# Four edits to the scans of a state-space layer: the order of sums, products, loads and splits

## The chip, the cores and the metric

The kernel runs on one core of a Trainium2 chip. The metric is the device time of one execution in microseconds (us). A profile of one execution gives each engine's instructions with start and duration. The engines are TensorE (PE), VectorE (DVE), ScalarE (ACT), GpSimd (POOL) and SyncE (SP, which here issues most of the DMAs). Each takes its own instructions strictly in order.

## The reference, cut to what matters

One inference step of two layers, a Mamba-2 layer and a pooling layer, over 1024 prompt tokens and 64 sample tokens (8 sequences of 8), in float32. The scans belong to the first layer:

```python
acum = jnp.cumsum(dt * A, axis=2)                         # per head, within chunks of 128 tokens
decay = where(mask, exp(acum[t] - acum[s]), 0)
y_intra = (C B^T * decay) @ (x * dt)                      # the rows of a chunk
chunk_states = B^T @ (x * dt * exp(acum[-1] - acum))      # what a chunk adds to the state
h_next = exp(acum[-1]) * h + chunk_states
y_inter = C @ h_prev * exp(acum)
y = y_intra + y_inter + d_skip * x
gated = y * silu(z)                                       # then normalised within each of 8 groups
gated = gated * rsqrt(mean(gated ** 2) + eps) * norm_g
out = gated @ w_out                                       # 2048 -> 1024
```

The 32 heads form 8 groups of 4 that share `B` and `C`. The prompt begins with a state of zero; each of the 8 sample sequences has a state of its own, read, used and returned.

## The kernel before, in words

All tensors lie feature-major: 128 features on the partitions, 1088 columns (1024 prompt tokens, 64 sample tokens). A product in nearly full precision takes three matmuls: each operand is split into a rounded part (`hh`, `wh`, `gh`) and a rest (`hl`, `wl`, `gl`). ScalarE makes the rounded part, VectorE the rest: for weights L141 and L145, for the out-projection's input `op_split`, L782 and L783.

The program has three stretches. The **front** (to about 348 us) has the normalisation, the modulation and a part of the in-projection; early in it the cumulative decays go to a DRAM tensor `acd`. Then **`ssd_layer`** runs eight scans, one for each group 0 to 7 (to about 925 us). Last comes the rest of the out-projection's layer and the pooling layer.

A scan is the generator `scan_group` (L521 ff.). For each of eight chunks of 128 tokens `front(c)` loads the decay of chunk c+2 into one of three `acb` tiles (`load_ac`, L549), broadcast to all partitions, 256 KB each; transposes `x` and `B` on TensorE into a bank `tr` (L573, L576); makes the decay matrix `M` on ScalarE, four times L581 and then an exponential L582, the row factor `ea` (L565), `cd` (L601), and `Bt`, the rounded transpose of `B` (L593). For each pair of chunks `states` makes the chunk states (`S`, L615) and `rows` the outputs (L637, L641), which VectorE adds to `x` (`evac_y`, L607). Chunk 8 is the sample: `sample_inter` multiplies the sample's `C` with the old states (`Z`, L656) and VectorE scales this (`zsc`, L659); `back_sample` adds to it on POOL (L665), multiplies with `M` (L670), and POOL scales the old states (L674, twice); `state_sample` makes four products `S[0]` to `S[3]` (L692), in banks of the kinds `S`, `y`, `y` and `tr`, and VectorE adds them to the states (L695, four times). Then come the products with `z` (L732), their squares on ScalarE (L733), the sum of the two squares on VectorE (`zsum`, L769), and in the scan's next step the row sums on TensorE (`ms`, L741). PSUM has two `tr` banks, two `y`, one `S` and three `mm`.

Between two steps of a scan, other work fills TensorE's queue, by a table `FILL` of unit counts: in the groups 0 to 4 units of the in-projection for the next groups (groups 1, 2, 3, 4 and 6, three `mm` banks evicted by ScalarE, L434 and L436, followed by a convolution over four taps, L366 to L372, most of it on VectorE), then units of the out-projection (`op_first`, L807 to L812). The very last in-projection unit (`proj_group`, group 6, part 3) also takes steps of a generator `prep`, each of which loads rows `gr` for the out-projection and splits the rows loaded before. A scheduler places the instructions on the engines by priority and readiness, so a changed order in the code can change it in a neighbouring place.

Of the kernel before, what the change touches and what calls it, by code (L numbers as in the profile page):

```python
# [11 lines left out]
ALU = mybir.AluOpType  # L12
# [3 lines left out]
P = 128  # L16
# [83 lines left out]
class Build:  # L100
# [296 lines left out]
    def proj_group(self, G):  # L397

        for ii in range(4):
            w = self.stream_next()  # L400
            raw = self.proj_begin(G, ii)
            if (G["g"], ii) == (BESIDE[-1], 3):

                ps = [self.mm_tile() for _ in CH]
                for k in range(8):
                    for c, j in ((0, k), (1, k), (2, 0), (2, k)) if k == 1 else ((0, k), (1, k), (2, k))[:3 if k else 2]:
                        self.mm1(ps[c], w, j, self.hn[j], CH[c], j == 0, j == 7)
                    for j in (0, 1) if k == 1 else (k,) if k else ():
                        self.slots.free(*self.hn[j])
                    if 0 < k < 5:  # L410
                        next(self.prep)
                    elif k in ():
                        self.load_x(0, k - 0)
                    if k < 7:
                        yield
                for c in range(3):
                    self.proj_evict(G, ii, raw, ps[c], c, False)
                next(self.prep)
                yield
                self.late = lambda: self.proj_end(G, ii, raw, True)  # L420
                return
            ada = self.ada_do(self.ada_plan[G["g"], ii]) if (G["g"], ii) in self.ada_plan else iter(())
            for c in range(3):
                ps = self.mm_tile()
                self.mm3(ps, w, self.hn, CH[c])
                self.proj_evict(G, ii, raw, ps, c)
                if c != (0, 0, 2, 0)[ii]:
                    next(ada, None)
                yield
# [95 lines left out]
    def scan_group(self, g, T):  # L525
        nc, tk, gp, pp = self.nc, self.tk, self.gs, self.pp
        B, C, xs, zs = T[0], T[1], T[2:4], []
        hsl, h0 = [], []

        def load_z():  # L530
            for q in range(2):
                zs.append(self.slots.get("z"))
                nc.sync.dma_start(zs[q], self.zsd[2 * g + q])

        def load_h0():
            for i in range(2):
                t = self.slots.get("h0")
                nc.sync.dma_start(t[:, :1024], self.io["h0T"][g][:, 1024 * i:1024 * i + 1024])
                hsl.append(t)
                h0.append(t[:, :1024].rearrange("p (b r q) -> p b r q", b=4, r=4))  # L540

        h = [None]
        acbs = {}

        def load_ac(c):
            if c < 8:
                j, cc = c // 2, c % 2
                t = gp.tile([P, 4, 128], F32, tag="acb", bufs=3, name=self.name("acb"))
                nc.sync.dma_start(t, self.acd[32 * j + 4 * g:32 * j + 4 * g + 4, 128 * cc:128 * cc + 128].unsqueeze(0).to_broadcast([P, 4, 128]))  # L549
            else:  # L550
                t = gp.tile([P, 4, 128], F32, tag="acb", bufs=3, name=self.name("acb"))[:, :, :64]
                nc.sync.dma_start(t, self.acd[96 + 4 * g:100 + 4 * g, 256:320].unsqueeze(0).to_broadcast([P, 4, 64]))
            acbs[c] = t
# [133 lines left out]
        def state_sample(xm, Bt):  # L687
            S = [pp.tile([P, 512], F32, tag=t, bufs=b, name=self.name("S")) for t, b in (("S", 1), ("y", 2), ("y", 2), ("tr", 2))]
            for i in range(2):
                for j in range(4):  # L690
                    o = slice(32 * j, 32 * j + 32)
                    nc.tensor.matmul(S[j], Bt[i][o, :], xm[o, :], start=(i == 0), stop=(i == 1), tile_position=(32 * j, 0))  # L692
            for j in (3, 2, 1, 0):
                d = hsl[j // 2][:, 512 * (j % 2):512 * (j % 2) + 512]
                nc.vector.tensor_tensor(out=d, in0=d, in1=S[j], op=ALU.add)  # L695
            for i in range(2):
                nc.sync.dma_start(self.io["hsT"][g][:, 1024 * i:1024 * i + 1024], hsl[i][:, :1024])
                self.slots.free(hsl[i])

        load_ac(0)  # L700
        load_ac(1)
        F = [front(0)]
        yield
        F.append(front(1))
        yield
        for c in range(0, 8, 2):
            states(c, F)
            if c == 6:
                load_z()
            Fn = [front(c + 2)]  # L710
            if c == 6:
                self.slots.free(B)
            yield
            rows(c, F)
            F = Fn
            if c < 6:
                F.append(front(c + 3))
                if c == 4:
                    load_h0()
            else:  # L720
                zsc = sample_inter()
                self.slots.free(C)
            yield
        F, h = F[0], h[-1]
        nc.sync.dma_start(self.io["hpT"][g], h.rearrange("p r q -> p (r q)"))
        st = back_sample(F, zsc)
        yield
        state_sample(*st)

        sq = zs  # L730
        for q in range(2):
# [1 line left out]
            nc.scalar.activation(sq[q], xs[q], AF.Square)  # L733
        self.zadd = functools.partial(nc.vector.tensor_tensor, out=sq[0], in0=sq[0], in1=sq[1], op=ALU.add)
        if g not in (5, 6):
            self.zsum()
        yield
        self.zsum()
        ps = self.pp.tile([P, 512], F32, tag="y", bufs=2, name=self.name("ms"))
# [745 lines left out]
    def front_pairs(self, ops, dt):  # L1485

        nc, sl = self.nc, self.slots
        self.fast_init(len(FRONT))
        self.G, G, ends = {}, None, []

        def end(G, g, ii, ts):
            for i in range(2):
                self.proj_end(G, ii + i, ts[i])
                if g:
                    t = G["out"].pop()
                    nc.sync.dma_start(self.xbd[g][ii + i], t)
                    sl.free(t)

        for n, (kind, g) in enumerate(FRONT):
            if kind == "z":  # L1500
                ts = [sl.get("z") for _ in range(2)]
                outs = [(t, 0, None) for t in ts]
            else:
                if kind == "b":
                    self.G[g] = G = self.proj_open(g)
                ii = 2 * (kind == "x")
                ts = [self.proj_begin(G, ii + i) for i in range(2)]
                outs = [(t, 3, t[:, 1027:1115].rearrange("p (b w) -> p b w", w=11)[:, :, 3:11]) for t in ts]

            def after(x):  # L1510
                if kind == "z" and x in ("z01", "z11"):
                    a = HALF * int(x[1])
                    self.z_chunk(ts[1], ts[1][:, a:a + HALF], a, HALF)
                elif kind == "z" and x in ("B21", "B22"):
                    a = HALF * (x == "B22")
                    ins = self.z_chunk(ts[0], ts[0][:, a:a + HALF], a, HALF)
                    if n == len(FRONT) - 1 and x == "B22":
                        with self.tc.issue_after(ins.ins):
                            t = self.mt.tile([P, NS], F32, tag="gs", bufs=2, name=self.name("gs"))
                            nc.scalar.activation(t[:, :1], self.eps, AF.Exp)  # L1520
                    if x == "B22":
                        self.gate_store(2 * g, ts[0])
                elif kind == "z" and x == "T4":
                    self.gate_store(2 * g + 1, ts[1])
                if x == "B21":
                    while ends:
                        ends.pop(0)()
                if kind != "z" and x == "B22":
                    ends.append(functools.partial(end, G, g, ii, ts))
                if n == 0 and x in ("B11", "B21"):  # L1530
                    next(ops)
                if n < 2 and x in ("B21", "T3", "T4"):
                    next(dt, None)
                if n == len(FRONT) - 1:
                    if x in ("T2", "T3"):
                        sl.free(*[self.T[int(x[1]), k] for k in range(4)])
                    elif x == "T1":
                        for k in range(4):
                            for i in range(2):
                                nc.sync.dma_start(self.hn[k][i][:, HALF:].bitcast(F32), self.b12d[2 * k + i])  # L1540

            self.fast_pair(*outs, after)
        for f in ends:
            f()
        sl.free(*[self.T[4, k] for k in range(4)])
# [366 lines left out]
```

## Time and profile before

| what | value |
| --- | --- |
| median of 3 runs | 1600.0 us (1599.32 to 1602.75) |
| the profiled execution's own time | 1601.08 us |
| its span in the trace | 1599.3 us |
| TensorE busy | 1572.6 us, 98% |
| VectorE, ScalarE, GpSimd busy | 81%, 49%, 32% |
| scans | about 348 to 925 us |

In rows of the timeline the columns are the start, the time to the end of the last of them, engine, line, operation, output and inputs, shapes, and how many were put together; in brackets stands the idle time of the engine before it and what ended that. In the list of waits each row names the engine and the operation that waited, the operation it waited for, the total, how often and the longest.

### The profile page before, as it was taken

The page shows a single profiled execution, that of the slowest core. Times are in us where ns is not written, and L with a number is a line of the kernel's source. Part 1 is how long each engine was busy: PE and PEld are TensorE (multiplying, and loading weights), DVE is VectorE, ACT ScalarE, POOL GpSimd, SP SyncE. Part 2 cuts the span into 40 slices and gives each one's busy share as a digit, 9 for nine tenths or more (in the row PEclk, how much of TensorE's full clock was granted, in tenths as well). Part 3 has the DMA queues.
Part 4 walks back from the last instruction along what each step waited for, and adds up shares of the span by engine and source line. Part 5 has one row for each costly group of instructions (what it writes and reads, how often), then busy time and mean ns, then how long its engine had stood idle before and what let it go on. Part 6 is the DMA issues. An engine that isn't in the chain of part 4 may idle for free.

```text
span 1599.3 us, 30704 instructions
## 1 busy us (share of the span) xinstructions
PE 1572.6 (98%) x11946; PEld 1505.4 (94%) x11946; DVE 1299.5 (81%) x2152; ACT 790.2 (49%) x1512; POOL 514.1 (32%) x558
## 2 busy tenths in 40 slices
PE   9999999999999999999999999999999999999997
PEld 7899999999898988888998999999999999999997
DVE  6874879778888888889888868998889777667886
ACT  6663344357666666675555437533332233233364
POOL 0133556512322313141211232375666630000241
PEclk9999999999999999999999999999999999999999
DMA  9422232355555654579989532232333379566683
GB/s 353 166 100 108 72 112 83 110 179 170 174 161 166 179 182 145 207 246 321 310 325 319 191 135 73 66 136 102 116 112 110 104 248 366 140 180 180 161 171 116
DMA packets 122306, 275.59 MB, mean 172 GB/s; under 512 B 18192, under 2 KB 59312, under 8 KB 122160
## 3 DMA queue, kind: packets, MB, share of 16 engines
q1 hardware_dynamic: 118128, 260.90, 47.7%
q0 software_dynamic: 4032, 12.72, 4.6%
q8 instruction: 94, 1.54, 0.4%
q14 instruction: 52, 0.43, 0.1%
HBM read 201.12 MB, written 70.23 MB: 170 GB/s over the span
## 4 chain that ended last, share of the span: by engine, by line
PE 79%; DVE 9%; issue 4%; ACT 4%; DMA 2%; POOL 1%; SPq 0%; DVEq 0%; ACTq 0%; POOLq 0%
PE st L1053 10%; PE st L1051 10%; PE st L1052 10%; PE mm L190 10%; PE mm L191 10%; PE mm L192 9%; PE op L1270 2%; PE op L1271 2%; PE op L1269 2%; PE S L615 2%; PE y L637 2%; DMA acb<-acd 1%; PE tr L576 1%; PE am L261 1%; PE tr L573 1%
## 5 line engine op out<-in xcount | busy, mean ns | idle before, releaser
L1051 PE MATMUL st<-hh,w 128*128 128x272 f32 x832 | 240.3, 289 | 0.9 <-ACT w L182 0.9
L1053 PE MATMUL st<-hh,w 128*128 128x272 f32 x832 | 240.4, 289 | 0.4 <-DVE w L184 0.4
L1052 PE MATMUL st<-hl,w 128*128 128x272 f32 x832 | 239.9, 288 | 0.0
L1051 PE MATMUL st<-t,w 128*128 128x272 f32 x624 | 179.6, 288 | 0.0
L1053 PE MATMUL st<-t,w 128*128 128x272 f32 x624 | 179.5, 288 | 0.0
L1052 PE MATMUL st<-t,w 128*128 128x272 f32 x624 | 179.2, 287 | 0.0
L190 PE MATMUL mm<-hh,wh 128*128 128x368 f32 (+1 forms) x528 | 178.2, 337 | 0.0
L191 PE MATMUL mm<-hl,wh 128*128 128x368 f32 (+1 forms) x528 | 174.8, 331 | 0.0
L192 PE MATMUL mm<-hh,wl 128*128 128x368 f32 (+1 forms) x528 | 173.2, 328 | 0.0
L1051 PEld LDWEIGHTS st<-hh,w 128*128 128x128 f32 x832 | 156.7, 188 | 1.3 <-ACT w L182 1.3
L1053 PEld LDWEIGHTS st<-hh,w 128*128 128x128 f32 x832 | 156.4, 188 | 0.9 <-DVE w L184 0.9
L1052 PEld LDWEIGHTS st<-hl,w 128*128 128x128 f32 x832 | 156.7, 188 | 0.0
L182 ACT ACTIVATE w<-wr 128x512 fp32r<-128x512 f32 x104 | 64.9, 629 | 166.4 <-PE st L1053 137.4
L623 POOL TENSOR_TENSOR hd<-h,cd 128x256 f32<-128x256 f32 x56 | 47.5, 849 | 303.2 <-DVE h L624 142.1
L1270 PE MATMUL op<-b,w 128*128 128x272 f32 x448 | 128.9, 288 | 1.0 <-DVE b L1199 1.0
L1269 PE MATMUL op<-b,w 128*128 128x272 f32 x448 | 129.4, 289 | 0.0
L1271 PE MATMUL op<-b,w 128*128 128x272 f32 x448 | 129.0, 288 | 0.1
L190 PE MATMUL mm<-gh,wh 128*128 128x368 f32 (+1 forms) x372 | 125.5, 338 | 0.0
L192 PE MATMUL mm<-gh,wl 128*128 128x368 f32 (+1 forms) x372 | 122.1, 328 | 0.0
L191 PE MATMUL mm<-gl,wh 128*128 128x368 f32 (+1 forms) x372 | 121.9, 328 | 0.1
L1051 PEld LDWEIGHTS st<-t,w 128*128 128x128 f32 x624 | 117.7, 189 | 0.1
L1053 PEld LDWEIGHTS st<-t,w 128*128 128x128 f32 x624 | 117.3, 188 | 0.0
(307 smaller groups left out, 4578.1 us busy)
## 6 DMA issues: line engine op xcount, KB each, us to landing
wr<-win SPq DMA_DIRECT2D x48, 512.0 KB, 3.6
acb<-acd SPq DMA_DIRECT2D x64, 256.0 KB, 4.4
wr<-pin SPq DMA_DIRECT2D x32, 512.0 KB, 3.7
wr<-pout SPq DMA_DIRECT2D x28, 512.0 KB, 5.4
x<-x1d SPq DMA_DIRECT2D x24, 544.0 KB, 6.0
x1d<-x SPq DMA_DIRECT2D x22, 544.0 KB, 4.3
wr<-pout POOLq DMA_DIRECT2D x20, 512.0 KB, 5.6
x<-xT SPq DMA_DIRECT2D x16, 544.0 KB, 6.3
```

What stands on the lines that cost most here:

```text
L182: self.nc.scalar.activation(hi, src, AF.Copy)
L190: nc.tensor.matmul(ps[:, :n], hi[:, k, :], ah[:, a:a + n], start=first, stop=False)
L191: nc.tensor.matmul(ps[:, :n], hi[:, k, :], al[:, a:a + n], start=False, stop=False)
L192: nc.tensor.matmul(ps[:, :n], lo[:, k, :], ah[:, a:a + n], start=False, stop=last)
L615: nc.tensor.matmul(S[:, 256 * i:256 * i + 256], Bt, xde.rearrange("p r q -> p (r q)"), start=True, stop=True)
L623: nc.gpsimd.tensor_tensor(out=hd, in0=h[-1], in1=cd.unsqueeze(2).to_broadcast([P, 4, 64]), op=ALU.mult)
L1051: nc.tensor.matmul(ps[c][:, :QUART], hi[:, k], xh[:, t], start=(k == 0), stop=False)
L1052: nc.tensor.matmul(ps[c][:, :QUART], hi[:, k], xl[:, t], start=False, stop=False)
L1053: nc.tensor.matmul(ps[c][:, :QUART], lo[:, k], xh[:, t], start=False, stop=(k == 3))
L1269: nc.tensor.matmul(ps[:, :QUART], hi[:, k], xh, start=k == 0, stop=False)
L1270: nc.tensor.matmul(ps[:, :QUART], hi[:, k], xl, start=False, stop=False)
L1271: nc.tensor.matmul(ps[:, :QUART], lo[:, k], xh, start=False, stop=k == 7)
```

## The change

Four things change, with no effect on what is computed.

1. In a scan, the sum of the two squares (`zsum`) is issued only after the last of the four additions to the sample's state has been placed (all groups but 5 and 6, where it already came later).
2. `sample_inter`, the product of the sample's `C` with the old states, is emitted ahead of the rows of the chunks 6 and 7 and no longer behind them.
3. The decays of the chunks 0 and 1 of scan 0 are loaded within the front into a slot `acs`, as soon as the last product of the front has given up some of its tiles; the scan then starts with chunk 2's load. The slot is given back after `front(1)`.
4. In the last in-projection unit (group 6, part 3), one step of `prep` moves from between the matmuls to behind the evictions.

```diff
@@ proj_group
-                    if 0 < k < 5:
+                    if 0 < k < 4:
                         next(self.prep)
...
                 for c in range(3):
                     self.proj_evict(G, ii, raw, ps[c], c, False)
+                next(self.prep)
                 next(self.prep)
                 yield
@@ state_sample
             for j in (3, 2, 1, 0):
                 d = hsl[j // 2][:, 512 * (j % 2):512 * (j % 2) + 512]
-                nc.vector.tensor_tensor(out=d, in0=d, in1=S[j], op=ALU.add)
+                ins = nc.vector.tensor_tensor(out=d, in0=d, in1=S[j], op=ALU.add)
...
+            return ins
@@ scan_group
-        load_ac(0)
-        load_ac(1)
+        acbs.update(self.ac01)
+        self.ac01 = {}
+        for c in range(2):
+            if c not in acbs:
+                load_ac(c)
         F = [front(0)]
         yield
         F.append(front(1))
+        if self.acsl is not None:
+            self.slots.free(self.acsl)
+            self.acsl = None
...
+            if c == 6:
+                zsc = sample_inter()
+                self.slots.free(C)
             rows(c, F)
...
-            else:
-                zsc = sample_inter()
-                self.slots.free(C)
...
-        state_sample(*st)
+        added = state_sample(*st)
...
         if g not in (5, 6):
-            self.zsum()
+            self.zsum(added)
@@ front_pairs, after product T3 of the last pair
+                        if x == "T3":
+                            self.acsl = t = sl.get("acs")
+                            self.ac01 = {c: t[:, 512 * c:512 * c + 512].rearrange("p (r t) -> p r t", r=4) for c in range(2)}
+                            for c in range(2):
+                                nc.sync.dma_start(self.ac01[c], self.acd[0:4, 128 * c:128 * c + 128].unsqueeze(0).to_broadcast([P, 4, 128]))
```

Three places in the engines' orders follow. The line numbers of the changed kernel are higher by 1 from L418 on and by 8 from L732 on.

VectorE at the end of group 3, before (`ea` is the row factor of a later group's chunk, `h` the sample's states, `S` the four products with `S_7552` to `S_7555` for `S[0]` to `S[3]`, `z` the squares, `wl` a weight's rest):

```order
L602 TENSOR_TENSOR ea_7834<-xbc_7167,ea_7834 128x512
L769 TENSOR_TENSOR z_7356<-z_7356,z_7358 128x1088
L695 TENSOR_TENSOR h_117_7313<-h_117_7313,S_7555 128x512
L695 TENSOR_TENSOR h_117_7313<-h_117_7313,S_7554 128x512
L695 TENSOR_TENSOR h_116_7311<-h_116_7311,S_7553 128x512
L695 TENSOR_TENSOR h_116_7311<-h_116_7311,S_7552 128x512
L280 TENSOR_SCALAR shf_275<-am_7541,vec 128x9
```

and now (`S_7551` to `S_7554` for `S[0]` to `S[3]`):

```order
L603 TENSOR_TENSOR ea_7833<-xbc_7166,ea_7833 128x512
L696 TENSOR_TENSOR h_117_7310<-h_117_7310,S_7551 128x512
L696 TENSOR_TENSOR h_118_7312<-h_118_7312,S_7553 128x512
L696 TENSOR_TENSOR h_118_7312<-h_118_7312,S_7554 128x512
L696 TENSOR_TENSOR h_117_7310<-h_117_7310,S_7552 128x512
L777 TENSOR_TENSOR z_7355<-z_7355,z_7357 128x1088
L280 TENSOR_SCALAR shf_275<-am_7540,vec 128x9
```

The sum of squares stands behind the additions, and the additions themselves now come as `S[0]`, `S[2]`, `S[3]`, `S[1]` where they came as `S[3]`, `S[2]`, `S[1]`, `S[0]`. It is so at the end of the groups 0 to 3; at the end of group 4 they keep the old order.

ScalarE at the start of scan 0, before (the tiles `acb_4131`, `acb_4133` and `acb_4135` are the decays of the chunks 0, 1 and 2; `raw` is an eviction of the in-projection):

```order
L593 ACTIVATE Bt_4153<-tr_4137 128x128
L434 ACTIVATE raw_4164<-mm_4167 128x368
L581 ACTIVATE M_4142<-acb_4131,tka_1447 128x128 x4
L565 ACTIVATE ea_4195<-acb_4133 128x512
L582 ACTIVATE M_4142<-M_4142 128x512
L581 ACTIVATE M_4202<-acb_4133,tka_1448 128x128 x4
L601 ACTIVATE cd_4215<-acb_4133 128x4
L434 ACTIVATE raw_4164<-mm_4218 128x368
L582 ACTIVATE M_4202<-M_4202 128x512
L593 ACTIVATE Bt_4213<-tr_4197 128x128
L565 ACTIVATE ea_4255<-acb_4135 128x512
```

and now (`acs_4022` holds the chunks 0 and 1, `acb_4134` chunk 2):

```order
L582 ACTIVATE M_4141<-acs_4022,tka_1447 128x128 x4
L594 ACTIVATE Bt_4152<-tr_4136 128x128
L583 ACTIVATE M_4141<-M_4141 128x512
L566 ACTIVATE ea_4194<-acs_4022 128x512
L435 ACTIVATE raw_4163<-mm_4166 128x368
L582 ACTIVATE M_4201<-acs_4022,tka_1448 128x128 x4
L602 ACTIVATE cd_4214<-acs_4022 128x4
L566 ACTIVATE ea_4254<-acb_4134 128x512
L583 ACTIVATE M_4201<-M_4201 128x512
L594 ACTIVATE Bt_4212<-tr_4196 128x128
```

Both chunks' `M` come from the new slot, and the row factor of chunk 2 (`ea_4254`), which was behind the second `Bt`, now stands two places ahead of it.

ScalarE at the end of group 4, before (`gh` are the rounded parts of rows for the out-projection, `z` the squares of the two halves, `raw` the evictions of the three banks of the last in-projection unit, `wh` a weight's rounded part):

```order
L782 ACTIVATE gh_8435<-gr_8418 128x1088
L733 ACTIVATE z_8232<-xbc_7414 128x1088
L782 ACTIVATE gh_8493<-gr_8433 128x1088
L601 ACTIVATE cd_8759<-acb_8589 128x4
L434 ACTIVATE raw_8342<-mm_8345 128x368
L434 ACTIVATE raw_8342<-mm_8346 128x368
L141 ACTIVATE wh_8503<-wr_8340 128x1024
L434 ACTIVATE raw_8342<-mm_8347 128x288
L436 ACTIVATE raw_8342<-mm_8347 128x8x8
L366 ACTIVATE raw_8779<-raw_8342,cwh 128x1112
L733 ACTIVATE z_8234<-xbc_7602 128x1088
```

and now:

```order
L741 ACTIVATE z_8231<-xbc_7413 128x1088
L790 ACTIVATE gh_8492<-gr_8486 128x1088
L435 ACTIVATE raw_8341<-mm_8344 128x368
L435 ACTIVATE raw_8341<-mm_8345 128x368
L741 ACTIVATE z_8233<-xbc_7601 128x1088
L435 ACTIVATE raw_8341<-mm_8346 128x288
L437 ACTIVATE raw_8341<-mm_8346 128x8x8
L141 ACTIVATE wh_8502<-wr_8339 128x1024
L366 ACTIVATE raw_8778<-raw_8341,cwh 128x1112
```

The weight's split `wh` moved from between the evictions to behind them; the fourth split of rows (`gh_8492`) is still ahead of the first eviction; the square of the second half (`z_8233`) came up from behind the evictions to ahead of the third one. On VectorE the second product with `z`, which that square reads, now stands behind the four additions, as it did.

## The prediction

> **What bounds the kernel now.** First the page's first part and the busy time by stage (columns: stretch, its length, then busy us of PE, PEld, DVE, ACT, POOL, granted clock, DMA share, GB/s).
>
> ```profile
> PE 1572.6 (98%) x11946; PEld 1505.4 (94%) x11946; DVE 1299.5 (81%) x2152; ACT 790.2 (49%) x1512; POOL 514.1 (32%) x558
> ...
> 361.00:421.00 60.00, 59.84 (x488) 54.09 (x486) 51.10 (x78) 42.68 (x105) 19.64 (x27) 1.00 0.55 160
> ...
> 700.00:727.00 27.00, 23.32 (x158) 21.03 (x151) 26.92 (x35) 20.05 (x35) 10.58 (x11) 1.00 0.77 259
> ```
>
> TensorE is busy 1572.6 of 1599.3 us at a clock of 1.00, and the change leaves its arithmetic alone. So only its idle 26.7 us can be won, and only the part in the scans: no edit touches what runs after 925. One stretch is different: from 700 to 727 VectorE is busy 26.92 of 27.00 us and TensorE loses 3.7 us. Next the waits of TensorE (us in total, times, longest).
>
> ```profile
> PE tr L573 <- DVE h L695: 3.6, 4, 1.0
> PE S L615 <- ACT Bt L593: 2.3, 4, 1.5
> PE y L670 <- POOL zsc L665: 2.1, 2, 1.2
> PE mm L807 <- ACT raw L434: 1.6, 1, 1.6
> ...
> PE ms L741 <- DVE z L769: 0.9, 1, 0.9
> ```
>
> These five are 10.5 us, and the four edits aim at them. Each is a wait for an engine that works through its own queue in order, so the question at each is whether the queue comes earlier, or only TensorE does.
>
> **Sum of squares behind the state's additions** (groups 0 to 4 and 7; it bears on a wait at the handovers 0 to 3). The next group's first transposes need the PSUM bank of `S[3]`, which an addition frees. VectorE and TensorE at the end of group 3, and the same transposes after groups 0, 1 and 2:
>
> ```profile
> 625.06 1.23 DVE L145 TENSOR_TENSOR wl<-wr,wh 128x1024 fp32r<-128x1024 f32 x1 [1.32 <-ACT wh L141]
> ...
> 628.27 0.42 DVE L659 TENSOR_TENSOR zsc<-Z,eap 128x256 f32<-128x256 f32 x1
> 628.61 1.37 DVE L368 SCALAR_TENSOR_TENSOR raw<-raw,cwh,raw 128x1112 f32<-128x1112 f32 x1
> 630.06 1.05 DVE L602 TENSOR_TENSOR ea<-xbc,ea 128x512 f32<-128x512 f32 x1
> 631.03 3.05 DVE L368 SCALAR_TENSOR_TENSOR raw<-raw,cwh,raw 128x1112 f32<-128x1112 f32 x1
> 634.00 0.46 DVE L607 SCALAR_TENSOR_TENSOR xbc<-xbc,vec,y 128x64 f32<-128x64 f32 x2
> 634.38 2.64 DVE L732 TENSOR_TENSOR xbc<-xbc,z 128x1088 f32<-128x1088 f32 x1
> ...
> 638.22 1.28 DVE L732 TENSOR_TENSOR xbc<-xbc,z 128x1088 f32<-128x1088 f32 x1
> 639.42 0.68 DVE L602 TENSOR_TENSOR ea<-xbc,ea 128x512 f32<-128x512 f32 x1
> 640.68 1.29 DVE L769 TENSOR_TENSOR z<-z,z 128x1088 f32<-128x1088 f32 x1 [0.58 <-ACT z L733]
> 641.89 2.47 DVE L695 TENSOR_TENSOR h<-h,S 128x512 f32<-128x512 f32 x4
> ```
> ```profile
> 421.51 0.38 PE L573 MATMUL tr<-xbc,xbc 128*128 128x128 f32 x1 [0.63 <-DVE h L695]
> 494.57 0.38 PE L573 MATMUL tr<-xbc,xbc 128*128 128x128 f32 x1 [0.85 <-DVE h L695]
> 567.90 0.38 PE L573 MATMUL tr<-xbc,xbc 128*128 128x128 f32 x1 [1.05 <-DVE h L695]
> 642.62 0.38 PE L573 MATMUL tr<-xbc,xbc 128*128 128x128 f32 x1 [1.04 <-DVE h L695]
> ...
> 647.15 0.44 PE L741 MATMUL ms<-z,ones 128*32 128x272 f32 x4
> ```
>
> Now the first addition starts at 641.89 and the transpose 0.73 later. Without the sum ahead, the additions can start when L602 is through, 0.60 after its start (as the four follow each other: 2.47 in all, 0.60 from start to start), at 640.02: 1.87 earlier (the wait of 0.58 and 1.29 of work, less overlap). That is more than any of the four waits. But the order printed above shows what the title does not say: in these groups the additions come in the order `S[0]`, `S[2]`, `S[3]`, `S[1]`, and the bank that TensorE wants is freed by the third, no longer by the first. Two additions are 1.20. The transpose is let go 1.87 − 1.20 = 0.67 earlier, at 641.95, and the rest of the wait stays: TensorE is ready at 642.62 − 1.04 = 641.58. The first handover gains its whole 0.63, the others 0.67 each at most: 0.63 + 3 × 0.67 = **2.6 us** of 3.6. The sum itself goes behind the additions, 641.89 + 2.47 − 1.87 = 642.5 to about 643.7; the row sums that read it come at 647.15 (last row), so it costs nothing there.
>
> **Sample product ahead of the last rows.** It moves `Z` (16 matmuls) before the rows in TensorE's queue, and `zsc` L659 ahead of a convolution and two evictions in VectorE's. The waits to be had:
>
> ```profile
> 630.61 0.28 PE L670 MATMUL y<-M,zsc 128*64 128x64 f32 x2 [0.90 <-POOL zsc L665]
> ...
> 628.84 1.72 POOL L665 TENSOR_TENSOR zsc<-zsc,xd 128x256 f32<-128x256 f32 x1 [1.88 <-DVE zsc L659]
> 630.52 5.35 POOL L674 TENSOR_TENSOR h<-h,es 128x1024 f32<-128x1024 f32 x2
> ```
>
> The second time is in group 4 (2.1 − 0.9 = 1.2). In group 3 `zsc` follows the weight split, at 626.2 for 628.27; POOL's addition ends near 628.5 and TensorE, due at 629.71, has no wait. The banks for that product are freed by two evictions of 0.4, the second behind one convolution of 1.37: near 628.8, 0.9 ahead. So 0.9 goes here, yet TensorE then meets the handover 0.9 earlier, and there VectorE's queue decides: between the split at 625.06 and the additions it has no idle time, so 641.95 stands, and the wait at the transposes grows to about 1.3. **I count 0 in group 3**; 0.9 if VectorE came earlier too. Group 4's 1.2 is counted with its end, below. POOL's two scalings L674 start 2 us earlier, which moves whom they hold up: beside them VectorE took 1.05, 3.05 and 2.64 for operations that elsewhere in these rows take 0.68, 1.37 and 1.28, 3.4 more. I take the same 3.4 afterwards, on other operations.
>
> [...]
>
> **First decay loads in the front.** Scan 0 now begins like this:
>
> ```profile
> 349.33 2.92 SPq L549 DMA_DIRECT2D acb<-acd  x3
> ...
> 355.78 1.28 ACT L581 ACTIVATE M<-acb,tka 128x128 f32<-128x128 f32 x4 [3.02 <-DMA acb<-acd]
> ...
> 360.15 0.25 ACT L593 ACTIVATE Bt<-tr 128x128 f32<-128x128 f32 x1
> ...
> 356.69 0.59 PE L615 MATMUL S<-xd,Bt 128*128 128x256 f32 x2
> 360.46 0.70 PE L615 MATMUL S<-xd,Bt 128*128 128x256 f32 x2 [1.52 <-ACT Bt L593]
> ```
>
> ScalarE waits 3.02 us for the first load, and the second `Bt`, queued behind two chunks of decay, is late. Afterwards both chunks lie ready, but in the order above the exponential of chunk 2 stands before the second `Bt`, and its load is the first of the queue, landing where the first landed now, near 355.8. Two operations later (about 0.6 each) `Bt` starts near 357.2; TensorE, with less work in between, is there at about 357.1. The wait of 1.52 shrinks to about 0.2: **1.3 us**; at most 1.5, and 0.3 if chunk 2 lands 1 us later. The 512 KB themselves and the two DMA issues are not new, only earlier; the stretch 361 to 421 moves 160 GB/s, so they have room.
>
> **One split behind evictions** (and all of group 4's end). ScalarE, VectorE and TensorE there:
>
> ```profile
> 716.13 0.83 ACT L434 ACTIVATE raw<-mm 128x368 f32<-128x368 f32 x2
> 719.64 1.10 ACT L733 ACTIVATE z<-xbc 128x1088 f32<-128x1088 f32 x1
> ...
> 715.87 2.47 DVE L695 TENSOR_TENSOR h<-h,S 128x512 f32<-128x512 f32 x4
> 718.26 1.28 DVE L732 TENSOR_TENSOR xbc<-xbc,z 128x1088 f32<-128x1088 f32 x1
> ...
> 716.65 0.43 PE L807 MATMUL mm<-gh,wh 128*128 128x368 f32 x1 [1.59 <-ACT raw L434]
> 718.38 0.43 PE L807 MATMUL mm<-gh,wh 128*128 128x352 f32 x1
> 723.15 0.67 PE L741 MATMUL ms<-z,ones 128*32 128x272 f32 x8 [0.86 <-DVE z L769]
> ```
>
> The fourth split still stands ahead of the first eviction in ScalarE's order; it is a weight split that went behind them. And the square of the second half now stands ahead of the third eviction, while its input, the second product L732, stands on VectorE behind the four additions. Replayed with these durations: additions 714.2 to 716.6, product to 717.8, square (1.10) to 718.9, third eviction to 719.5, where 718.38 was; the first out-projection tile near 716.95 for 716.65. The third tile is 1.1 late, the row sums' 0.86 wait goes: **−0.2 us**, and the 1.2 of `zsc` only makes TensorE wait longer for the evictions. Bounds: if VectorE frees its queue 3 us sooner all three waits go, +3.7; if the second product is itself held up (2.64 for 1.28), −1.6.
>
> **Sum.** 2.6 + 1.3 − 0.2 = 3.7. The profiled execution took 1601.08 (span 1599.3): 1597.4. It lies 1.08 above the median of the runs shown, 1600.0, so the forecast against the median is **1596.3**.
>
> **Rivals.** *Scalings in full*: the two L674 take at least 1.93 each (row below), 3.86 for the 3.4 counted; each handover then gains 0.2, not 0.67. [...] 0.8 + 1.3 − 0.2 = 1.9: **1598.1**.
>
> ```profile
> L674 POOL TENSOR_TENSOR h<-h,es x16: 1927/2387/3014, 409.4 to 902.6; 128x1024 f32<-128x1024 f32 x16
> ```
>
> *The waits go whole*: VectorE's queue comes earlier by what TensorE gains, for instance because the scalings fall on evictions. 3.6 + 0.9 + 1.3 = 5.8, and group 4 up to 3.7 more: **1594.2** down to 1590.5. Against: no idle time on VectorE between 625 and 640.
>
> *The change does not do what it says*: the second queue at each place (ScalarE's in the front, VectorE's at the handovers) keeps the old dates: **1600.0**. For: two of four edits visibly leave another instruction in the way. Against: 0.58 of pure waiting leaves VectorE's queue.
>
> *Slower*: the earlier scalings hold up one more convolution per group, ahead of the second eviction. Its place is VectorE between the split and the additions, its price 3.05 − 1.37 = 1.68 in each of the groups 0 to 3; it decides from where POOL's first scaling begins before that convolution (by the replay 628.5 against 627.0, so not). First the 0.9 of margin at `y` is eaten, then each transpose comes 1.68 later than forecast: 1596.3 + 4 × 1.68 = **1603.0**.
>
> **Chances.** Forecast 0.48 (own range 1595.2 to 1597.3: each of the terms off by a third); scalings in full 0.19; whole waits 0.17; nothing 0.07; slower 0.09. A difference under 0.2%, 3.2 us, cannot be told from none. Faster than that: the whole waits and three quarters of the forecast, 0.53. Same: the rest of the forecast, scalings in full, nothing: 0.38. Slower 0.09. The range 1592.5 to 1600.2 leaves out the slower case and the far half of the whole waits.
>
> **What would show it.** In the waits of TensorE: `tr` on the additions still there, with some 0.4 after group 2 and 1.3 after group 3, and the third addition just ahead of it; `y` on `zsc` gone; the second `S` of scan 0 under 0.4; the out-projection's first tile waiting about 3 us on an eviction; no wait of the row sums. On VectorE no wait ahead of the additions. The forecast falls if the `tr` waits vanish (better), if L674's neighbours lose more than 3.4 in a group, or if a wait appears at `y`.

## The result and the profile after

The changed kernel took 1596.61 us (median of 13 runs, 1593.88 to 1599.48), the kernel before 1600.89 beside it (13 runs, 1599.32 to 1603.71). The ratio is 0.9971, with a 95% interval of 0.9963 to 0.9980: 0.2% to 0.4% faster, some 4.6 us. Forecast were 1596.3 us and "faster". The profiled execution of the change took 1598.18 us (span 1596.4), 1.6 above its median; two later profiles of the same code have spans of 1594.1 and 1593.1. So single places are read from three executions below, not from one.

The waits of TensorE after the change (us in total, times, longest), to be laid beside those quoted in the prediction:

```profile
PE S L616 <- ACT Bt L594: 2.6, 4, 1.4
PE mm L815 <- ACT raw L435: 2.0, 1, 2.0
PE am L270 <- ACT mp L266: 1.2, 3, 0.5
...
PE tr L574 <- DVE h L696: 0.7, 2, 0.4
...
PE ms L749 <- DVE z L777: 0.2, 1, 0.2
```

The transposes' wait fell from 3.6 to 0.7 and did not vanish; `zsc` is gone from the list; the wait for the evictions grew from 1.6 to 2.0; and the total at the chunk states `S`, which the loads in the front were to cut, is 2.6 where it was 2.3.

**The handover after group 3** (VectorE, then TensorE):

```profile
622.82 1.23 DVE L145 TENSOR_TENSOR wl<-wr,wh 128x1024 fp32r<-128x1024 f32 x1 [1.32 <-ACT wh L141]
...
624.68 1.76 DVE L368 SCALAR_TENSOR_TENSOR raw<-raw,cwh,raw 128x1112 f32<-128x1112 f32 x1
...
626.76 2.66 DVE L368 SCALAR_TENSOR_TENSOR raw<-raw,cwh,raw 128x1112 f32<-128x1112 f32 x1
629.34 2.43 DVE L603 TENSOR_TENSOR ea<-xbc,ea 128x512 f32<-128x512 f32 x1
631.70 1.36 DVE L368 SCALAR_TENSOR_TENSOR raw<-raw,cwh,raw 128x1112 f32<-128x1112 f32 x1
...
637.04 0.68 DVE L603 TENSOR_TENSOR ea<-xbc,ea 128x512 f32<-128x512 f32 x1
637.64 2.47 DVE L696 TENSOR_TENSOR h<-h,S 128x512 f32<-128x512 f32 x4
...
639.57 0.38 PE L574 MATMUL tr<-xbc,xbc 128*128 128x128 f32 x1 [0.36 <-DVE h L696]
```

The additions follow the last `ea` by 0.60, with no wait between. The transpose comes 639.57 − 637.64 = 1.93 behind the first addition, where it was 0.73 before: two additions more. From the split to the additions VectorE now needs 637.64 − 622.82 = 14.82; before it needed 641.89 − 625.06 = 16.83. Beside POOL three operations of VectorE are longer, 1.76 for 1.37, 2.66 for 1.37 and 2.43 for 0.68: 3.43 together, on other operations than before, where it was 3.41. The first of them stands beside the end of POOL's addition to `zsc` (624.53 to 625.27), only the other two beside the scalings.

**The start of scan 0** (ScalarE, then TensorE):

```profile
354.67 0.63 ACT L566 ACTIVATE ea<-acb 128x512 f32<-128x512 f32 x1 [0.29 <-DMA acb<-acd]
...
355.73 0.26 ACT L594 ACTIVATE Bt<-tr 128x128 f32<-128x128 f32 x1
...
363.45 0.21 ACT L602 ACTIVATE cd<-acb 128x4 f32<-128x4 f32 x1 [3.43 <-DMA acb<-acd]
...
371.41 1.13 ACT L369 ACTIVATE raw<-raw 128x1112 f32<-128x1112 f32 x1 [0.77 <-DVE raw L368]
372.44 0.64 ACT L594 ACTIVATE Bt<-tr 128x128 f32<-128x128 f32 x2
...
356.61 1.02 PE L616 MATMUL S<-xd,Bt 128*128 128x256 f32 x4
372.76 0.70 PE L616 MATMUL S<-xd,Bt 128*128 128x256 f32 x2 [1.37 <-ACT Bt L594]
```

The second chunk state now stands right behind the first (four matmuls in one go from 356.61) and waits for nothing. But the fourth one, at 372.76, waits 1.37, where before it had no wait. ScalarE stands 3.43 us before chunk 5's decay, which lands at 363.45, and behind that `cd` wait a weight split, two evictions, the convolution and the fourth `Bt`.

**The end of group 4** (TensorE and ScalarE; then the busy time of 3-us stretches, whose third number from the right is the granted clock):

```profile
713.69 0.43 PE L815 MATMUL mm<-gh,wh 128*128 128x368 f32 x1 [1.99 <-ACT raw L435]
...
713.18 0.82 ACT L435 ACTIVATE raw<-mm 128x368 f32<-128x368 f32 x2
714.75 1.11 ACT L741 ACTIVATE z<-xbc 128x1088 f32<-128x1088 f32 x1 [0.75 <-DVE xbc L740]
```
```profile
711.00:714.00 3.00, 1.01 (x7) 0.72 (x6) 3.00 (x6) 2.95 (x6) 0.00 (x0) 1.00 0.86 254
714.00:717.00 3.00, 3.00 (x12) 3.00 (x11) 3.00 (x3) 2.25 (x5) 0.77 (x1) 0.51 1.04 409
717.00:720.00 3.00, 3.00 (x18) 2.75 (x17) 3.00 (x5) 1.43 (x2) 2.65 (x2) 0.92 0.95 293
```

The first out-projection tile waits 1.99 for its bank, the row sums no longer wait, and behind the wait TensorE runs at half its clock for some 3 us, which no forecast had.

### The profile page after: what moved, and what is told of

It is laid out like the page before. It is cut to its first block, busy times and chain, and to the rows that moved or that the text cites. A ratio compares the mean times of both kernels' runs of the same rounds, so it can differ in the third digit from the quotient of the medians.

```text
span 1596.4 us, 30712 instructions
## 1 busy us (share of the span) xinstructions
PE 1573.5 (99%) x11946; PEld 1506.6 (94%) x11946; DVE 1299.4 (81%) x2152; ACT 790.1 (49%) x1512; POOL 519.4 (33%) x558
## 3 DMA queue, kind: packets, MB, share of 16 engines
q8 instruction: 94, 1.54, 0.4%
## 4 chain that ended last, share of the span: by engine, by line
PE 79%; DVE 8%; issue 4%; DMA 4%; ACT 4%; POOL 1%; SPq 0%; DVEq 0%; ACTq 0%; POOLq 0%
PE st L1061 10%; PE st L1059 10%; PE st L1060 10%; PE mm L190 10%; PE mm L191 9%; PE mm L192 9%; PE op L1278 2%; PE op L1279 2%; PE op L1277 2%; DMA acb<-acd 2%; PE S L616 2%; PE y L638 2%; DVE raw L368 1%; PE tr L577 1%; DVE xbc L359 1%
```

## The experiments

Twelve runs followed, two of them of the changed kernel again, each beside the kernel before. Medians in us, and ratios with 95% intervals:

| kernel | median us | before | ratio |
| --- | --- | --- | --- |
| sum of squares alone | 1597.37 | 1600.35 | 0.9982 (0.9973 to 0.9991) |
| sample product alone | 1601.12 | 1600.35 | 1.0008 (0.9998 to 1.0017) |
| loads in the front alone | 1600.27 | 1600.35 | 0.9997 (0.9988 to 1.0006) |
| split alone | 1600.33 | 1600.35 | 0.9995 (0.9985 to 1.0004) |
| sum and sample product | 1596.65 | 1600.50 | 0.9980 (0.9971 to 0.9989) |
| whole, without the sample product | 1595.55 | 1600.50 | 0.9976 (0.9967 to 0.9985) |
| whole, second time | 1595.58 | 1599.95 | 0.9968 (0.9956 to 0.9981) |
| whole, third time | 1596.47 | 1600.50 | 0.9976 (0.9967 to 0.9985) |
| whole, `tr` bank first | 1596.48 | 1599.95 | 0.9979 (0.9969 to 0.9989) |
| whole, evictions first | 1597.44 | 1599.95 | 0.9980 (0.9970 to 0.9989) |
| both of these | 1597.17 | 1599.95 | 0.9977 (0.9964 to 0.9989) |
| whole, slot held longer | 1595.14 | 1600.50 | 0.9969 (0.9958 to 0.9980) |

Beside them stands how far a kernel is ahead of the profiled execution of before, in us, at the same matmul (the chunk states of the scans, one profile each; the traces differ by 0.1 to 0.6 before the change begins):

```
                        whole   2nd    3rd   sum alone  slot held
scan 0, first S          0.07  0.59   0.42     0.54       0.36
scan 0, fourth S         0.66  0.55   0.67     0.03       1.86
group 0, late            0.68  0.55   0.86     0.23       1.86
group 1, first S         1.34  1.24   1.54     0.72       2.72
group 1, late            1.47  1.39   1.69     0.87       2.87
group 2, first S         1.19  1.80   2.10     0.19       2.65
group 2, late            1.20  1.79   2.09     0.18       2.64
group 3, first S         2.49  2.55   2.90     1.21       4.08
group 3, late            2.38  2.89   3.38     1.55       3.34
group 4, first S         3.05  5.13   5.59     3.32       4.39
group 4, late            2.57  5.00   5.14     2.74       3.74
group 5, first S         2.47  4.83   5.76     3.32       4.50
```

A step from "late" to the next "first S" is a handover.

### The sum of squares alone

```diff
...
-        state_sample(*st)
+        added = state_sample(*st)
...
-            self.zsum()
+            self.zsum(added)
```

> Only the sum of squares goes behind the additions. Theory (the third addition frees the bank that TensorE wants): the four handovers gain 0.63 + 3 x 0.67 = 2.6 us, and waits of the transposes on the additions of 0.2 to 0.4 us stay after groups 1, 2 and 3; the waits for zsc (2.1 us) and at group 4's end are as before. Rival (the waits go whole): 3.6 us and no such wait left. Rival (nothing): 0.

Measured: ratio 0.9982, 2.9 us (1.4 to 4.3). VectorE from the split to the additions, the transposes after the groups 1, 2 and 3, and the waits that were left:

```profile
622.38 1.23 DVE L145 TENSOR_TENSOR wl<-wr,wh 128x1024 fp32r<-128x1024 f32 x1 [1.32 <-ACT wh L141]
...
637.37 2.47 DVE L695 TENSOR_TENSOR h<-h,S 128x512 f32<-128x512 f32 x4
...
494.38 0.38 PE L573 MATMUL tr<-xbc,xbc 128*128 128x128 f32 x1 [0.36 <-DVE h L695]
566.66 0.49 PE L573 MATMUL tr<-xbc,xbc 128*128 128x128 f32 x2 [0.21 <-DVE h L695]
639.29 0.49 PE L573 MATMUL tr<-xbc,xbc 128*128 128x128 f32 x2 [0.36 <-DVE h L695]
```
```profile
PE y L670 <- POOL zsc L665: 1.8, 2, 1.0
```

637.37 − 622.38 = 14.99, against 16.83: the queue is 1.84 shorter, where 1.87 was worked out. The waits of 0.36, 0.21 and 0.36 are those of the third addition. One edit makes the larger part of the whole change's gain. The other three measured nothing alone (1.0008, 0.9997 and 0.9995), so the 1 to 2 us that the whole change has above it are not put down to any of them.

### The sample product alone, and everything but it

```diff
+            if c == 6:
+                zsc = sample_inter()
+                self.slots.free(C)
             rows(c, F)
...
-            else:
-                zsc = sample_inter()
-                self.slots.free(C)
```

> Only the sample product goes ahead of the last rows. Theory (VectorE's queue sets the handovers): the two waits for zsc, 2.1 us, vanish, but the transposes after group 3 wait about 0.9 longer and the evictions at group 4's end about 1.2 longer, so 0 to 0.3 us in all. Rival (the waits go whole): 2.1 us. Rival (slower): the scalings hold up one more operation per group, 4 x 1.7 us lost.

> The whole change without the edit on the sample product. Independent edits: 2.9 us (the sum's), as loads and split gave nothing alone; waits for zsc of 1 to 2 us are back. If the sample product is worth what the waits for zsc were, 2 us more time than the whole change.

> Only the two edits on the sum of squares and on the sample product. Alone they gave 1597.4 and 1601.1 against 1600.35: if they act independently, both together give some 2 to 3 us and the rest of the whole change's 4.4 us comes from the loads and the split. Rival (they need one another: with the sum out of VectorE's way the wait for zsc is really won, without it the transposes' wait takes it back): 4 us or more.

Measured: alone 1.0008, so nothing gained. Without it the whole change keeps 0.9976, exactly the ratio of the whole change on the same chip. Sum and sample product together, 0.9980, are not better than the sum alone, 0.9982. So this edit is worth nothing that these runs can tell, alone or beside the others. Group 4 of the kernel without it shows why:

```profile
699.89 0.28 PE L671 MATMUL y<-M,zsc 128*64 128x64 f32 x2 [0.97 <-POOL zsc L666]
...
711.84 0.44 PE L815 MATMUL mm<-gh,wh 128*128 128x368 f32 x1 [1.54 <-ACT raw L435]
```

0.97 at `zsc` and 1.54 at the evictions; with the edit 0 and 2.0. Half of what is won at the first is waited for at the second, 2.0 − 1.54 = 0.5, and behind the longer wait the clock fell to half in two of the three profiles of the whole change (below).

### The loads in the front, alone and with the slot held longer

> Only the first two decay rows are loaded in the front. My prediction said 1.3 us. The trace of the whole change says 0.6: the wait of 1.52 at the second chunk state goes, and one of 1.37 comes 14 us later, at the fourth, since ScalarE stands 3.4 us before a later load and the convolution that its queue then reaches is no earlier than it was.

Measured: 0.9997, nothing. The fourth chunk state and the stretches behind it:

```profile
373.47 0.48 PE L615 MATMUL S<-xd,Bt 128*128 128x256 f32 x1 [2.40 <-ACT Bt L593]
```
```profile
373.00:376.00 3.00, 2.53 (x11) 2.48 (x12) 2.62 (x5) 0.69 (x3) 0.90 (x1) 0.79 0.06 19
376.00:379.00 3.00, 3.00 (x30) 1.59 (x30) 1.02 (x2) 1.25 (x4) 1.09 (x2) 0.64 0.01 3
```

The wait moved here and is 2.40 in this execution, with the clock down behind it. To test its cause, the decays of the chunks 4 and 5 go into the new slot too:

```diff
-            load_ac(c + 2) if c < 7 else None
+            if acsv and c in (2, 3):
+                acbs[c + 2] = acsv[c - 2]
+                nc.sync.dma_start(acsv[c - 2], self.acd[64:68, 128 * (c - 2):128 * (c - 2) + 128].unsqueeze(0).to_broadcast([P, 4, 128]))
+            elif c < 7:
+                load_ac(c + 2)
...
-        if self.acsl is not None:
-            self.slots.free(self.acsl)
-            self.acsl = None
         yield
...
                 F.append(front(c + 3))
+                if c == 2 and self.acsl is not None:
+                    self.slots.free(self.acsl)
+                    self.acsl = None
```

> The whole change, with the new slot held longer: the decays of the chunks 4 and 5 of scan 0 go into it as well, so that their loads no longer wait for a buffer. Theory (ScalarE stands 3 to 4 us before chunk 5's load, and the fourth chunk state is late for that): that load lands before 361, the wait of 1.4 to 2.4 us at the fourth chunk state goes, and with it the drop of the clock where it came; 1.4 us under the whole change, up to 3 in executions with the drop. Rival (the queue of loads sets it): the wait stays, no difference.

```profile
360.47 0.21 ACT L606 ACTIVATE cd<-acs 128x4 f32<-128x4 f32 x1 [0.90 <-POOL hd L628]
...
362.00 0.21 ACT L606 ACTIVATE cd<-acs 128x4 f32<-128x4 f32 x1 [1.16 <-POOL hd L628]
```

ScalarE no longer waits for the load there, and the wait at the fourth chunk state is gone: this execution is 1.86 ahead at that place, the three of the whole change 0.55 to 0.67. The cause is shown. In the time it is 1595.14 against 1596.47 for the whole change on the same chip (ratios 0.9969 and 0.9976, intervals that overlap): about the 1.3 us of the trace, but not separable.

### The split alone, and the evictions first

> Only one step of the out-projection's loading goes behind the evictions. In ScalarE's order the fourth split stays ahead of the first eviction and the square of the second half comes up ahead of the third. Theory: TensorE's first out-projection tile waits as before (about 1.6 us), the third tile comes up to 1.1 us later and the row sums' wait of 0.9 goes: within 0.3 us of before. Rival (the split really frees the evictions): 1.6 us faster.

Measured: 0.9995 (0.9985 to 1.0004), no difference that can be told. In its profile the first tile still waits 1.4 us for an eviction (1.6 before), so the evictions were not freed. Then the whole change, with group 4's squares and the last two splits behind the three evictions (and the sum of these squares behind them):

```diff
                 for c in range(3):
-                    self.proj_evict(G, ii, raw, ps[c], c, False)
-                next(self.prep)
-                next(self.prep)
+                    ins = self.proj_evict(G, ii, raw, ps[c], c, False)
+                with self.tc.issue_after(ins.ins):
+                    next(self.prep)
+                    next(self.prep)
+                    self.zsq()
...
-        if g not in (5, 6):
+        if g not in (4, 5, 6):
             self.zsum(added)
```

> The whole change, with the squares and the last two splits of group 4 placed behind the three evictions in ScalarE's order. Theory (the evictions stand behind ScalarE's queue, and the clock drops because TensorE stands still): the wait of 2.0 us falls under 0.5, the clock stays at 1.00, and the time falls by 1.5 us (wait alone) to 3 us (with the clock) against the change. Rival (the next in line is as late): a wait of the row sums or of the fourth split takes its place, under 0.5 us gained.

```profile
PE mm L829 <- DVE gl L800: 2.4, 2, 1.6
```

The 2.0 at the first tile is gone and the clock stays at 1.00, but the rests `gl` of the two splits are now late on VectorE: two waits of 1.6 and 0.8 take the place. The ratio is 0.9980, no better than the whole change's 0.9968 on that chip. The rival holds.

### The bank of the transposes first

```diff
-                ins = nc.vector.tensor_tensor(out=d, in0=d, in1=S[j], op=ALU.add)
+                with self.tc.issue_after(ins.ins) if j < 3 else contextlib.nullcontext():
+                    ins = nc.vector.tensor_tensor(out=d, in0=d, in1=S[j], op=ALU.add)
```

> The whole change, with the four additions kept in their old order, so that the bank of the next transposes is freed by the first. Theory (the third addition holds them): the waits of the transposes on the additions, 0.7 us in the trace of the change, vanish, and the time falls by up to 0.7 us against the change. Rival (another wait stands behind it, ScalarE's product before L270): no difference.

> Both: additions in the old order and evictions first. If the two are independent, the gains of the two runs add up: 1.5 to 3.7 us under the change.

Measured: the transposes' waits are gone from the list, as the theory of the third addition says. The time is not better: 0.9979 and, for both edits together, 0.9977, with 0.9968 for the whole change beside them. 0.7 us is below what these runs tell apart, and in the profile of either the wait at scan 0's fourth chunk state was 2.2 to 2.3 us, 0.9 above the 1.37 of the first profile, with the clock down behind it (0.69 and 0.50 from 373 to 376 us): the wait alone took more than that.

### The whole change again

> The whole change once more, for a second profile. If TensorE's clock drops to half for some 3 us after its wait of 2.0 us at group 4's end in each execution, the profile shows granted clock near 0.5 there again, matmuls at 0.31 us from start to start instead of 0.17, and the section ends 2.5 us ahead of before. If that was a chance of one execution, the clock is 1.00 there and the section ends about 4 us ahead.

> The whole change a third time, beside the others on one chip: 1595 to 1597 us. A third look at the wait of 2.0 us at group 4's end: if such a wait always brings the clock down, granted clock near 0.5 to 0.8 for 3 us behind it; if it depends on where the wait falls, 1.00 is possible, and the time is then about 1.5 us less.

Measured: 0.9968 and 0.9976. Group 4's end in the third profile:

```profile
710.92 0.43 PE L815 MATMUL mm<-gh,wh 128*128 128x368 f32 x1 [2.01 <-ACT raw L435]
```
```profile
711.00:714.00 3.00, 2.18 (x13) 1.99 (x13) 3.00 (x3) 2.25 (x5) 0.54 (x1) 1.00 1.02 405
714.00:717.00 3.00, 3.00 (x27) 2.64 (x25) 3.00 (x5) 1.67 (x2) 2.89 (x2) 1.00 1.01 283
```

The same wait, and the clock stays up; in the second profile it was at half from 712.00 to 715.41, in the first from 714.06 to 717.47. From this matmul to the row sums it took 716.73 − 710.92 = 5.81 here, 6.31 in the first profile and 6.54 in the second. So the drop cost 0.5 to 0.7 at this place, not the 1.5 expected: without it TensorE waits 0.8 for the third eviction instead.

The large difference between the three profiles is the handover after group 3: 0.67 in the first, 2.24 and 2.21 in the others. VectorE in the third, and ScalarE's waits for two decay loads of the next scan in the first, in the third, and before:

```profile
620.27 1.23 DVE L145 TENSOR_TENSOR wl<-wr,wh 128x1024 fp32r<-128x1024 f32 x1 [1.62 <-ACT wh L141]
...
635.09 2.47 DVE L696 TENSOR_TENSOR h<-h,S 128x512 f32<-128x512 f32 x4
```
```profile
617.70 0.21 ACT L602 ACTIVATE cd<-acb 128x4 f32<-128x4 f32 x1 [2.17 <-DMA acb<-acd]
618.95 0.21 ACT L602 ACTIVATE cd<-acb 128x4 f32<-128x4 f32 x1 [1.04 <-DMA acb<-acd]
```
```profile
615.25 0.21 ACT L602 ACTIVATE cd<-acb 128x4 f32<-128x4 f32 x1 [1.22 <-DMA acb<-acd]
616.10 0.21 ACT L602 ACTIVATE cd<-acb 128x4 f32<-128x4 f32 x1 [0.65 <-POOL hd L624]
```
```profile
619.87 0.21 ACT L601 ACTIVATE cd<-acb 128x4 f32<-128x4 f32 x1 [1.95 <-DMA acb<-acd]
621.19 0.21 ACT L601 ACTIVATE cd<-acb 128x4 f32<-128x4 f32 x1 [1.11 <-DMA acb<-acd]
```

635.09 − 620.27 = 14.82, the very length of the first profile (14.81 in the second and with the slot held, 14.98 and 14.99 in the two kernels with the sum but without the sample product). What differs is where it begins: the weight split on VectorE waits for ScalarE's half, and ScalarE stands before two decay loads, the second of which lands at 618.95 in the one and is no longer waited for in the other. TensorE was 1.0 earlier there than in the first profile (3.38 against 2.38 ahead), the queue 2.55 earlier, and the waits at `zsc` and at the transposes were both won.

The difference is older than these two loads, though: in the first profile the first of them was issued at 613.11, in the third at 611.01. Before that ScalarE stands at `es`, which reads the sample's decay (the issue of that load and the end of the wait, in the first profile and in the third):

```profile
596.63 0.37 SPq L553 DMA_DIRECT2D acb<-acd  x1
603.05 0.27 ACT L570 ACTIVATE es<-acb 128x32 f32<-128x32 f32 x1 [3.35 <-DMA acb<-acd]
```
```profile
596.22 0.37 SPq L553 DMA_DIRECT2D acb<-acd  x1
600.97 0.26 ACT L570 ACTIVATE es<-acb 128x32 f32<-128x32 f32 x1 [1.68 <-DMA acb<-acd]
```

From issue to `es` it took 6.42 in the first profile, 4.75 in the third, 4.56 in the second: the same code. In the profile of before it took 6.31. So the second and the third are compared with a profile in which this load was slow, and not all of their 2.2 belongs to the edits: the split alone, which leaves VectorE's queue as it was, had 4.53 there and gained 1.4 at this handover (0.92 to 2.30 ahead). Why one load takes so differently long stays open.

## Why the prediction was right, and where it was not

**Time, sign and range** were right: 1596.3 forecast, 1596.61 measured, gain 3.7 forecast and 4.6 (3.2 to 5.9) measured. That the sum fits so well is in part luck: the loads gave less than the 1.3 counted, and the handovers in two of three profiles more than their 2.6.

**The third addition** was right. Waits of 0.2 to 0.4 stayed at the transposes as worked out, they went when the bank came first, and the queue's own shortening was 1.84 for 1.87. The term of 2.6 for the four handovers, with 0 for `zsc`, measured 2.3 in the first profile (0.66 − 0.28 + 1.29 + 0.67 in the table), 4.1 in the second and the third, and 2.6 with the sum alone. The single handovers in these went from −0.68 to 2.24, where at most 0.63 or 0.67 each was counted, so the totals agree better than their parts. After group 3 the step "VectorE's queue decides, so 641.95 stands" took the split at 625.06 as given, but that is set by ScalarE before decay loads. In the first profile, where the sample's decay was about as slow as before, this handover gained 0.67, just what was counted; in the other two it gained some 1.5 more. The wait of 1.3 forecast after group 3 was 0.36, with another 0.37 ahead of it at L270, where TensorE waits for ScalarE.

**The sample product at 0** was right, and so was its reason in group 4: there its 1.2 goes to the evictions. The 3.4 counted for the scalings came out as 3.43. But it was not all theirs: the operation of 1.05 before (0.68 elsewhere) stands beside the end of POOL's addition to `zsc`, as the one of 1.76 does now, 0.37 and 0.39. Beside the scalings themselves VectorE lost 3.04 both times, 0.82 less than the 3.86 of the rival "scalings in full". That the whole length of both goes to VectorE's queue was the author's estimate, and no run shows it. One eviction from PSUM stood between the two convolutions while the first scaling ran (626.37, behind POOL's start at 625.23). It was no longer than others, 0.47 with a median of 0.47 over all 80 of its line, and took 0.39 of VectorE's time, start to start, about half of the 0.82; the rival had left it out. The other half is not explained.

**The loads, 1.3**, were mis-sized. The second `Bt` came at 355.73 and TensorE did not wait there, a little better than forecast. What failed is that the step ended with the wait removed. It didn't ask what ScalarE reaches next: chunk 5's load, whose buffer comes free only when chunk 2 is done. The fourth chunk state then waits 1.4 to 2.4. From the first chunk state to the fourth the three profiles gained 0.59, −0.04 and 0.25; alone the edit measured 0.5 us (−1.0 to 1.9).

**Group 4's end, −0.2**: from the last rows of group 4 to group 5 the three profiles went −0.10, −0.17 and +0.62. The order was read rightly (square and split ahead of the evictions), the wait of the first tile was forecast as about 3 and was 2.0, and the row sums' wait went. The alone run, 0.9995, agrees with a term near nothing.

**The rivals**: "the waits go whole" has the handover after group 3 right in two profiles of three, but VectorE's queue came earlier there with a load that landed sooner, and the split alone shows such a gain without the edit; for group 4 it does not hold. "Scalings in full", with its 1.9 us, "nothing" and "slower" lie outside the interval of the ratio.

## What to carry to other kernels

When a wait goes, follow the queue of the engine that was waited for to the next thing that engine itself waits for: here a buffer's load behind the one that was brought forward gave most of the gain back 12 us later. The length of a queue between two points was the same to 0.04 us (14.81 to 14.85) in all eight profiles with both the sum's and the sample product's edit, while its start moved by over 2 us, and the trail led back to the landing of one load some 20 us earlier; so a forecast from a queue needs both, the length from the rows and the start from what released it. And read the order of the instructions that were not meant to move: the third addition in place of the first cost 1.2 of the 1.87 that the edit freed.

## What the hardware showed that was not expected

After some waits of about 2 us TensorE's clock fell to half for 3.41 us. These are all waits over 1.9 us in the scans of the fourteen profiles; the column of windows is explained below.

```
                                                         most idle us
kernel                     place                 wait us in a window   half clock
whole                      group 4's end          1.99     1.99        yes
whole, second              group 4's end          2.01     2.01        yes
whole, third               group 4's end          2.01     1.65        no
sample product alone       scan 0, second S       2.29     2.29        yes
sample product alone       group 4's end          2.02     2.02        yes
loads alone                scan 0, fourth S       2.40     2.13        yes
bank first                 scan 0, fourth S       2.23     2.23        yes
bank first                 group 4's end          2.01     1.58        no
both                       scan 0, fourth S       2.32     1.95        yes
sum and sample product     group 4's end          2.24     1.31        no
slot held                  group 4's end          2.01     1.42        no
```

Seven of eleven were followed by a drop; single waits of 1.2 to 1.8 never were. The length alone does not decide: of five waits of 2.01 and 2.02 two were followed by a drop. What separates them in these rows is where the wait falls. In the first profile the record of the granted clock begins at 4.09; the clock falls at 714.06, 709.97 or 208 × 3.413 later, rises at 717.47, one further on, and falls at 1591.28, 256 further on. In "sample product alone" it falls at about 361.5, 498.0 and 719.9, which is 40 and 65 times 3.413 apart. Cut into windows of this length, each profile from its own changes of the clock, the wait of the first profile lies in one window (idle 3.41 − 1.42 = 1.99), that of the third in two (0.36 and 1.65):

```profile
710.65:714.06 3.41, 1.42 (x9) 1.13 (x8) 3.41 (x6) 3.30 (x6) 0.00 (x0) 1.00 0.89 274
714.06:717.47 3.41, 3.41 (x14) 3.41 (x13) 3.41 (x4) 2.72 (x5) 1.24 (x1) 0.50 1.04 402
```
```profile
705.86:709.27 3.41, 3.05 (x19) 2.76 (x17) 3.41 (x5) 3.37 (x7) 0.00 (x0) 1.00 0.90 313
709.27:712.68 3.41, 1.76 (x10) 1.64 (x10) 3.41 (x5) 2.66 (x5) 0.00 (x0) 1.00 0.96 319
```

Every window of the scans in which TensorE was idle for 1.95 us or more, eight in all, was followed by one at half clock. Two further drops stood behind two shorter waits in close sequence. In "both" (1.59 and 0.77) the two fell into one window, with 1.99 idle; in "evictions first" the same two fell into two, with 1.46 and 0.89, and the clock stayed up. In "sample product alone" (0.36 and 1.04) the window had only 1.40 idle, and windows with up to 1.71 elsewhere left the clock up, so idle time alone does not sort them all. At half clock a matmul of 368 columns started 0.31 after the one before, else 0.17. In this kernel, 98% busy, a wait of 2 us thus cost more than its length where it fell into one window (0.5 to 0.7 more at group 4's end), and two shorter waits in one window (1.59 and 0.77) were followed by the same drop.
